# Decode pages taken in pairs, with another order of key and value pages beside the prompt

## The chip, the cores and the metric

The kernel runs on one core of one Trainium2 chip. The metric is device time in microseconds (us) of one execution; the figure shown is the median of the runs, and the lowest and highest beside it. A profile is one execution recorded instruction by instruction. The engines are PE (matrix multiply; PEld is its weight load), DVE (vector), ACT (activation), POOL (which also issues the gathers) and SP (which issues most other transfers).

## The reference

One step of a hybrid decoder layer for two groups that share the weights: a prompt of 1024 rows, and 8 samples of one row each with a cache of 8192 past positions in 64 pages of 128.

```python
# per layer, for the prompt (xp) and the samples (xs)
q, k, v, logf, u, z = mixer_inputs(rmsnorm(x, g_mix), w_in, b_f, g_sgu_v)
# prompt: causal attention with forget gates; samples: the same over the paged cache
s = einsum('bqhd,bkhd->bhqk', q, k) * HEAD_DIM ** -0.5 + (cq - ck)
att = einsum('bhqk,bkhd->bqhd', softmax(s), v)
x = x + concat(rmsnorm(att), rmsnorm(u * spatial(z))) @ w_o
# cross-attention, 4 heads of 256, into 256 memory rows (the samples' are cached)
x = x + cross_attend(rmsnorm(x, g_cross), mk, mv, w_cq, w_co)
# gated MLP with a causal convolution of width 3 over rows
h = rmsnorm(x, g_ffn) @ w_up
x = x + (silu(gate(conv(h))) * value(conv(h))) @ w_down
y = rmsnorm(x, g_final)
```

D_MODEL is 1024, there are 8 attention heads of 64 and D_FF is 2816. The outputs are both groups' rows, and the new keys, values, gates, memory keys and values and convolution states.

## The kernel before

Two streams of work are woven into one program. The first, `prompt()`, is a generator that goes through the prompt: `p1` (the input projection, and at its end the first loads of the attention), `attention(0)` beside the memory's keys and values (`pmem`) and the gating, `attention(1)`, and then for each half of 512 rows the merge, the output projection, the cross-attention (`cross`) and the MLP (`ffn`). Its large products are three whole-array matmuls each of 512 columns (`gemm3`, lines 271 to 273: high by high, high by low, low by high part). Weights come by SP into `wr`, ACT makes the high part `wh` (line 234) and DVE the low part `wl` (line 235).

The second stream, `sample()`, is the decode. `decode()` goes through the 8 samples' caches, 16 chunks each of 128 x 2048 numbers (1 MB), called pages here. A key page (`kstep`, line 1341) is gathered by POOL, multiplied by the query and summed on DVE (lines 1347 and 1351). When a sample's 16 key pages are done, its softmax follows (`soft_max`, `soft_all`, `soft_exp`, `soft_sum`). A value page (`vstep`, line 1400) is gathered by POOL, and PE multiplies it by the weights in four 32-column strips at once (line 1406). `sample_rest` then does the rest of the layer for the 8 rows, with weights and cached memory streamed as 1 MB pages too (`sample_proj`; cached keys and values at lines 1571 and 1606; `w_up` at 1652 with its matmuls at 1656; `w_down` at 1690 with its matmuls at 1695). All these pages share four buffers, `kv` (`NKV = 4`).

The loop at the end of `build` weaves the two: each step of `prompt()` yields an estimate of its PE time, and when the sum since the last decode step is over `PACE[phase]`, one step of the decode is emitted. `held[0]` stops that. A decode step in the order before is one key page and, one sample and two chunks behind, one value page; value pages are gathered one to a step and their matmuls emitted when two are pending (`VB = 2`). `behind(engine)` ties an instruction to come after the prompt's latest one on that engine. In the end a scheduler places the emitted instructions on the engines' in-order queues by what is ready and by order of emission, so that two pages emitted together need not stand together.

Of the kernel before, what the change touches and what calls it, by code (L numbers as in the profile page):

```python
# [18 lines left out]
P = 128  # L19
D = 1024  # L20
# [29 lines left out]

NKV = 4
VLAG = 2
VB = 2
MIXR = 1.0
G0R = 0.0
WH = 5
# [17 lines left out]
KS = 2  # L74
BKQ = 1
LA = (2, 2)
PACE = {'p1': 7.0, 'att0': 20.0, 'mid0': 8.0, 'ffn0': 8.5, 'att1': 15.0, 'mid1': 6.8, 'ffn1': 2.5, 'rest': 2.9}


def build(nc, tc, ctx, a, phases=None):  # L80
# [250 lines left out]
        return next(i for i in reversed(nc.cur_bb.bb.instructions) if i.engine == e)  # L331


    def p1(early):
        rstd = const.tile([P, 8], F32, tag="rstd", name="rstd")
        rstd8 = const.tile([P, 8], F32, tag="rstd8", name="rstd8")
# [203 lines left out]
        for tt in range(8):  # L540
            if tt < 4:
                ps = BK()
                mm_chunk(tt, ws, ps, 0, 512)
                if tt == SD - 1:
                    sps = [sample_copy(*sps[0])]
                if tt == SD:
                    sp = sample_sum(*sps[0])
                    zs = T2()[:8]
                    nc.scalar.activation(zs, sp, AF.Gelu_apprx_tanh, scale=rsk)
                    ssv = sm([8, 1], "sss", 1)  # L550
                    ssq_into(ssv, zs)
# [24 lines left out]
            nc.scalar.dma_start(zg_d[tt * P : (tt + 1) * P, :], z)  # L576
            yield 5.2 if tt < 4 else 0.1
# [104 lines left out]
    def attention(hf, late=None, at=3):  # L682
# [161 lines left out]
        for hp in range(4):  # L844
# [5 lines left out]
            for blk in range(2):  # L850
# [84 lines left out]
    def merge(att, sg):  # L935
# [12 lines left out]
        mh = mh[4:] + mh[:4]  # L948
        ml = ml[4:] + ml[:4]
        return mh, ml  # L950

    held = [False]

    def squares():
        return sm([P, 4, 2], "sqx", 2)
# [323 lines left out]
        yield 1  # L1279

    last = {}
    bgs, acc, phase = [], [0.0], ["p1", None]

    def behind(e):

# [3 lines left out]
    def decode():  # L1289
# [107 lines left out]
        def vstep(b, ch, st, dv):  # L1397
# [2 lines left out]
            nc.gpsimd.indirect_dma_start(kv, None, a["cache_v"], off(kidx[:, b, ch : ch + 1]))  # L1400
            kvv = kv.rearrange("p (k c) -> p k c", c=512)

            def mm():
                with behind(ENG.PE):
                    for j in range(4):
                        mmul(  # L1406
                            dv[32 * j : 32 * j + 32, :],
                            s[:, ch * 4 : ch * 4 + 4, :].rearrange("p k h -> p (k h)"),
                            kvv[:, j, :],
                            start=(ch == 0),  # L1410
                            stop=(ch == 15),
                            tile_position=(0, 32 * j),
                        )

# [21 lines left out]


        st, A, dt_, pm, dg, lp, dv, vm = ([None] * 8 for _ in range(8))
        pend = []
        st[0] = prep(0)  # L1440
        for g in range(8 * 16 + 16 + VLAG + 2):
            b, ch = divmod(g, 16)
            if ch == VLAG + 1 and 2 <= b < 10:
                vend(b - 2, vm[b - 2])
            if ch == 0 and 1 <= b < 9:
                dg[b - 1] = soft_all(b - 1, pm[b - 1])
            if ch == 1 and 1 <= b < 9:
                lp[b - 1] = soft_exp(b - 1, st[b - 1], dg[b - 1])
            if ch == 2 and 1 <= b < 9:
                soft_sum(b - 1, lp[b - 1])  # L1450
            if b < 8:
                kstep(b, ch, st[b])
# [8 lines left out]
            if len(pend) == VB:  # L1461

                for vb_, vch_, f in pend:
                    f()
                pend.clear()
                if vch_ == 15:
                    vm[vb_] = vmask(vb_, dv[vb_])
            vb, vch = divmod(g - 16 - VLAG, 16)
            if 0 <= vb < 8:
                if vch == 0:  # L1470
                    dv[vb] = DV()
                pend.append((vb, vch, vstep(vb, vch, st[vb], dv[vb])))
            yield 1


# [43 lines left out]
    def sample_rest(xs):  # L1519
# [81 lines left out]
            )  # L1601
        yield 1
        po = DV()
        for b in range(8):
            kv = KV().rearrange("p (a c) -> p a c", c=D)
            nc.gpsimd.dma_start(kv, a["cmv"][b].rearrange("(a p) c -> p a c", p=P))
            for n in range(2):
                for mt in range(2):
                    j = n * 2 + mt
                    mmul(po[32 * j : 32 * j + 32, :], pz[:, mt, b, :], kv[:, mt, n * 512 : (n + 1) * 512], start=(b == 0), stop=(b == 7), tile_position=(0, 32 * j))  # L1610
            yield 1
        vm = D2()
        nc.vector.tensor_tensor(
            vm.rearrange("p (h d) -> p h d", d=256),
# [28 lines left out]
        up = MS()  # L1643
        folds = []
        for f4 in range(11):
            ps = DV()
            for q in range(2):
                if q and folds:
                    folds.pop()()
# [3 lines left out]
                rv = raw.rearrange("p (f k c) -> p k f c", f=2, c=P)  # L1653
                for k in range(8):
                    j = k % 4
                    mmul(  # L1656
                        ps[32 * j : 32 * j + 32, q * 256 : (q + 1) * 256].rearrange("p (f c) -> p f c", f=2),
                        xsT[:, k, :],
                        rv[:, k],
                        start=(k < 4),  # L1660
                        stop=(k >= 4),
                        tile_position=(0, 32 * j),
                    )
                yield 1
            t = D2()
            nc.scalar.activation(t, ps, AF.Copy)

# [17 lines left out]
        nc.vector.tensor_tensor(g[:, :176], g[:, :176], hc[:, 176:352], op=ALU.mult)  # L1685
        yield 1
        ys = [DV(), MS()]
        for f2 in range(0, NF, 2):
            raw = KV().rearrange("p (f d) -> p f d", f=2)
            nc.gpsimd.dma_start(raw, a["w_down"][f2 * P : (f2 + 2) * P, :].rearrange("(f p) d -> p f d", p=P))  # L1690
            for q in range(2):
                f = f2 + q
                j = f % 4
                for n in range(2):
                    mmul(
                        ys[n][32 * j : 32 * j + 32, :],
                        g[:, f * 8 : f * 8 + 32],
                        raw[:, q, n * 512 : (n + 1) * 512],
                        start=(f < 4),
                        stop=(f >= NF - 4),  # L1700
                        tile_position=(0, 32 * j),
                    )
# [219 lines left out]
```

## Time and profile before

| | |
|---|---|
| median of 3 runs | 1874.07 us (1871.21 to 1876.5) |
| the profiled execution | 1881.57 us, its span 1879.7 us |
| mean granted TensorE clock | 0.982 |
| moved by DMA | 521.27 MB, mean 277 GB/s |

The span is from the first instruction to the last. A line of instructions reads: line of the kernel, engine, operation, tile written <- tiles read, shape, number, then total busy time, mean duration in ns, idle time of that engine just before such instructions, and what ended most of it. Matmuls overlap in the records, so the time that one costs is read from the start of one to the start of the next. Page matmuls are recorded as two instructions each.

### The profile page before, as it was taken

Reading aid. Unit: us, or ns where it says so; the run is one execution under the profiler, and the core shown is the slowest. Engines: PE = TensorE matmul, PEld = TensorE weight load, DVE = VectorE, ACT = ScalarE, POOL = GpSimd, SP = SyncE. Lnnn points to the kernel's source line nnn. Section 1 sums busy time; section 2 is a strip of 40 time slices with the busy share of each in tenths; the row PEclk is TensorE's granted clock in tenths of the full one; section 3 lists DMA queues with packets and bytes.
Section 4 is the critical chain, followed back from the end, with each engine's and each line's share of the span. In section 5 each row is a group of like instructions: output and inputs, shape, how many; then the busy total and the mean of one; then the engine's idle time right before and its main releaser. Section 6 shows DMA issues by size and latency. Waiting matters only on the chain.

```text
span 1879.7 us, 24248 instructions
## 1 busy us (share of the span) xinstructions
PE 1802.3 (96%) x9239; PEld 1291.7 (69%) x9239; DVE 1394.2 (74%) x1664; ACT 750.9 (40%) x1363; POOL 480.0 (26%) x437
## 2 busy tenths in 40 slices
PE   8999989878998999999999999999999999999998
PEld 5987666556676667776777776765675668667765
DVE  4788668776687787989989998897965549654344
ACT  6332356565633435333324234235353334232232
POOL 1232333331122332313422323334322111101110
PEclk9999999889998999999999999999999999999999
DMA  8877888784496876759877888889859577667971
GB/s 320 286 261 271 324 324 297 243 263 167 169 376 216 329 268 249 298 197 363 314 274 301 302 316 324 347 325 340 325 220 359 193 282 263 253 219 276 331 246 59
DMA packets 157012, 521.27 MB, mean 277 GB/s; under 512 B 20808, under 2 KB 40520, under 8 KB 124128
## 3 DMA queue, kind: packets, MB, share of 16 engines
q0 software_dynamic: 57168, 341.14, 49.1%
q1 hardware_dynamic: 92816, 165.99, 25.7%
q10 hardware_dynamic: 6912, 12.59, 1.8%
q8 instruction: 73, 1.20, 0.2%
q14 instruction: 43, 0.35, 0.1%
HBM read 495.73 MB, written 23.93 MB: 276 GB/s over the span
## 4 chain that ended last, share of the span: by engine, by line
PE 83%; DVE 5%; DMA 4%; ACT 3%; issue 3%; POOL 1%; SPq 0%; DVEq 0%; POOLq 0%; ACTq 0%
PE ba L271 13%; PE ba L272 12%; PE ba L273 12%; PE bb L271 7%; PE bb L272 7%; PE bb L273 7%; PE dv L1406 6%; DVE kv L1347 1%; PE dv L1656 1%; PE ba L1002 1%; PE ba L1004 1%; DMA kv<-cache_k,kidx 1%; PE bb L788 1%; DVE s L1351 1%; PE ba L1003 1%
## 5 line engine op out<-in xcount | busy, mean ns | idle before, releaser
L234 ACT ACTIVATE wh<-wr 128x1024 fp32r<-128x1024 f32 (+2 forms) x220 | 228.7, 1044 | 518.2 <-PE ba L272 168.5
L235 DVE TENSOR_TENSOR wl<-wr,wh 128x1024 fp32r<-128x1024 f32 (+2 forms) x220 | 262.8, 1200 | 134.0 <-PE ba L273 55.4
L1347 DVE TENSOR_TENSOR kv<-kv,d 128x1024 f32<-128x1024 f32 (+1 forms) x184 | 295.8, 1633 | 24.3 <-DMA kv<-cache_k,kidx 23.6
L1341 POOL DMA_INDIRECT kv<-cache_k,kidx x128 | 177.0, 1383 | 535.0 <-DVE s L1351 262.2
L1351 DVE TENSOR_REDUCE s<-kv 128x16 f32<-128x1024 f32 (+1 forms) x184 | 296.3, 1624 | 0.2
L1400 POOL DMA_INDIRECT kv<-cache_v,kidx x128 | 173.3, 1354 | 404.7 <-DVE s L1351 180.0
L271 PE MATMUL ba<-wh,u 128*128 128x512 f32 (+1 forms) x601 | 229.6, 383 | 4.3 <-DVE u L961 2.5
L272 PE MATMUL ba<-wl,u 128*128 128x512 f32 (+1 forms) x601 | 227.5, 379 | 0.0
L273 PE MATMUL ba<-wh,u 128*128 128x512 f32 (+1 forms) x601 | 224.9, 379 | 0.0
L272 PE MATMUL ba<-u,wh 128*128 128x512 f32 (+2 forms) x520 | 203.1, 391 | 0.0
L271 PE MATMUL ba<-u,wh 128*128 128x512 f32 (+2 forms) x520 | 202.7, 391 | 0.2 <-DVE u L238 0.2
L273 PE MATMUL ba<-u,wl 128*128 128x512 f32 (+2 forms) x520 | 202.1, 389 | 0.0
L271 PE MATMUL bb<-u,wh 128*128 128x512 f32 (+2 forms) x344 | 138.9, 404 | 1.1 <-DVE u L238 1.1
L271 PEld LDWEIGHTS ba<-wh,u 128*128 128x128 f32 x601 | 113.3, 189 | 38.2 <-issue 9.6
L272 PE MATMUL bb<-u,wh 128*128 128x512 f32 (+2 forms) x344 | 137.5, 401 | 1.6 <-DVE u L238 1.6
L1406 PE MATMUL dv<-kv,s 128*32 128x512 f32 x1024 | 135.2, 614 | 3.0 <-DMA kv<-cache_v,kidx 3.0
L273 PE MATMUL bb<-u,wl 128*128 128x512 f32 (+2 forms) x344 | 136.9, 398 | 0.0
L273 PEld LDWEIGHTS ba<-wh,u 128*128 128x128 f32 x601 | 113.0, 188 | 26.7 <-issue 5.0
L272 PEld LDWEIGHTS ba<-wl,u 128*128 128x128 f32 x601 | 113.3, 189 | 22.4 <-issue 1.7
L272 PEld LDWEIGHTS ba<-u,wh 128*128 128x128 f32 x520 | 98.5, 189 | 32.3 <-issue 12.2
L271 PEld LDWEIGHTS ba<-u,wh 128*128 128x128 f32 x520 | 98.3, 190 | 31.5 <-issue 8.4
L273 PEld LDWEIGHTS ba<-u,wl 128*128 128x128 f32 x520 | 98.2, 189 | 27.7 <-issue 8.1
(426 smaller groups left out, 3048.8 us busy)
## 6 DMA issues: line engine op xcount, KB each, us to landing
wr<-w_up SPq DMA_DIRECT2D x88, 512.0 KB
kv<-w_up POOLq DMA_DIRECT2D x22, 1024.0 KB
wr<-w_down SPq DMA_DIRECT2D x40, 512.0 KB
kv<-w_down POOLq DMA_DIRECT2D x11, 1024.0 KB
wr<-w_in SPq DMA_DIRECT2D x16, 512.0 KB
wr<-w_o SPq DMA_DIRECT2D x16, 512.0 KB
wr<-w_cq SPq DMA_DIRECT2D x16, 512.0 KB
wr<-w_co SPq DMA_DIRECT2D x16, 512.0 KB
```

The source lines that it names most:

```text
L234: nc.scalar.activation(h, src, AF.Copy)
L235: nc.vector.tensor_tensor(l, src, h.bitcast(F32), op=ALU.subtract)
L271: mmul(out, sh, mh, start=(i == 0), stop=False)
L272: mmul(out, sh, ml, start=False, stop=False)
L273: mmul(out, sl, mh, start=False, stop=(i == n - 1))
L788: nc.tensor.transpose(tr[:, c * P : (c + 1) * P], p_[:, kt * P : (kt + 1) * P], ident)
L1002: mmul(pss[i], mh[k][:, tb], wh, start=(k == korder[0]), stop=False)
L1341: nc.gpsimd.indirect_dma_start(kv, None, a["cache_k"], off(kidx[:, b, ch : ch + 1]))
L1347: nc.vector.tensor_tensor(kvv[:, i : i + m, :], kvv[:, i : i + m, :], qb.unsqueeze(1).broadcast_to((P, m, 512)), op=ALU.mult)
L1351: nc.vector.tensor_reduce(s[:, ch * 4 + i : ch * 4 + i + m, :].rearrange("p k h -> p (k h)"), kvv[:, i : i + m, :].rearrange("p k (h d) -> ...
L1400: nc.gpsimd.indirect_dma_start(kv, None, a["cache_v"], off(kidx[:, b, ch : ch + 1]))
L1406: mmul(dv[32 * j : 32 * j + 32, :], s[:, ch * 4 : ch * 4 + 4, :].rearrange("p k h -> p (k h)"), kvv[:, j, :], start=(ch == 0), stop=(ch == ...
```

## The change

- The decode no longer takes a key and a value page in each step. It counts key pages (`nk`) and value pages (`nv`) by themselves. In the phases named in `PATTERN` a letter chooses: `p1` takes keys alone, the first attention k v k k v, the second v v k (a v is a pair of value pages). In the other phases each step takes a key page and every second one also a pair of value pages.
- A pair's two gathers are issued in one step; in the next step the second page's matmuls are emitted, and the first page's tied to come right behind them (`first(newest(ENG.PE))`). The accumulation's start and stop move to chunks 1 and 14 to fit that order.
- `held[0]` is set at the projection's fifth tile of the last block, ahead of the attention's first loads, and cleared in the first attention at head pair 0, second block, first head, first row block, with the accumulated time set to 0. A `kstep` emitted while it is held is split in two.
- `PACE` is smaller in `p1` (6.3 for 7.0), `att0` (8.5 for 20), `ffn0` (8.0 for 8.5), `att1` (8 for 15) and `mid1` (6.7 for 6.8).
- In `sample_rest` the cached values, `w_up` and `w_down` are taken two pages at a time as well, the later first. For `w_down` all matmuls of one output half of both pages come together.

```diff
-VB = 2
+PATTERN = {'p1': 'k', 'att0': 'kvkkv', 'att1': 'vvk'}
+LINK = 1
-PACE = {'p1': 7.0, 'att0': 20.0, 'mid0': 8.0, 'ffn0': 8.5, 'att1': 15.0, 'mid1': 6.8, 'ffn1': 2.5, 'rest': 2.9}
+PACE = {'p1': 6.3, 'att0': 8.5, 'mid0': 8.0, 'ffn0': 8.0, 'att1': 8, 'mid1': 6.7, 'ffn1': 2.5, 'rest': 2.9}
...
                 if tt == 4:
+                    held[0] = True
                     early()
...
+                        if hf == 0 and (hp, blk, j, ii) == (0, 1, 0, 0):
+                            held[0], acc[0] = False, 0.0
...
-            def mm():
-                with behind(ENG.PE):
+            def mm(after=None):
+                with tc.issue_after(after) if after else behind(ENG.PE):
...
-                            start=(ch == 0),
-                            stop=(ch == 15),
+                            start=(ch == 1),
+                            stop=(ch == 14),
...
+        while nv < 128 or pend or ends:
+            k = nk < 8 * 16 + LINK + 3
+            v = nv < 128 and nk >= (nv // 16 + 1) * 16 + LINK + 2
+            if phase[0] in PATTERN:
+                p = PATTERN[phase[0]]
+                k = k and (not v or p[n % len(p)] == "k")
+                v = v and not k
+            elif n % 2:
+                v = False
+            if nk % 16 == 14 and nv - 2 * len(pend) < nk - 30:
+                k = False
+            n += 1
...
+            if k:
+                keys(*divmod(nk, 16))
+                nk += 1
+            if pend:
+                vb, vch, first, second = pend.pop()
+                second()
+                first(newest(ENG.PE))
...
+            if v:
+                vb, vch = divmod(nv, 16)
+                if vch == 0:
+                    dv[vb] = DV()
+                pend.append((vb, vch, *(vstep(vb, c, st[vb], dv[vb]) for c in (vch, vch + 1))))
+                nv += 2
             yield 1
...
+            for b in (b0 + 1, b0):
+                with tc.issue_after(newest(ENG.PE)) if b == b0 else nullcontext():
...
+            for q in (1, 0):
+                with nullcontext() if q else tc.issue_after(newest(ENG.PE)):
...
-        for f2 in range(0, NF, 2):
+        for f4 in range(0, NF, 4):
...
+            behind_ = None
+            for n in range(2):
+                for f2 in reversed(range(len(raws))):
+                    with tc.issue_after(behind_) if behind_ else nullcontext():
+                        for q in range(2):
+                            f = f4 + f2 * 2 + q
...
+                    behind_ = newest(ENG.PE)
```

`keys(b, ch)` is the old step's key part: the softmax steps of the sample before at chunks `LINK` to `LINK + 2`, then `kstep`, the gates at chunks 11 and 13, the next sample's query at 14 and `soft_max` at 15.

More of the change, by code (lines that the diff above doesn't have):

```diff
@@ L1281, in build @@
     last = {}
-    bgs, acc, phase = [], [0.0], ["p1", None]
+    bgs, phase = [], ["p1", None]
     def behind(e):
@@ L1438, in decode, with keys @@
         st, A, dt_, pm, dg, lp, dv, vm = ([None] * 8 for _ in range(8))
-        pend = []
+        pend, ends = [], []
         st[0] = prep(0)
[L1441 to L1445, printed above, removed]
+        nk = nv = n = 0
+        def keys(b, ch):
+            if ch == LINK and b:
                 dg[b - 1] = soft_all(b - 1, pm[b - 1])
-            if ch == 1 and 1 <= b < 9:
+            if ch == LINK + 1 and b:
                 lp[b - 1] = soft_exp(b - 1, st[b - 1], dg[b - 1])
-            if ch == 2 and 1 <= b < 9:
+            if ch == LINK + 2 and b:
                 soft_sum(b - 1, lp[b - 1])
@@ L1603, in sample_rest @@
         po = DV()
[L1604 to L1611, printed above, removed]
+        for b0 in range(0, 8, 2):
+            kvs = []
+            for b in (b0, b0 + 1):
+                kvs.append(KV().rearrange("p (a c) -> p a c", c=D))
+                nc.gpsimd.dma_start(kvs[-1], a["cmv"][b].rearrange("(a p) c -> p a c", p=P))
+            for b in (b0 + 1, b0):
+                with tc.issue_after(newest(ENG.PE)) if b == b0 else nullcontext():
+                    for n in range(2):
+                        for mt in range(2):
+                            j = n * 2 + mt
+                            mmul(
+                                po[32 * j : 32 * j + 32, :],
+                                pz[:, mt, b, :],
+                                kvs[b - b0][:, mt, n * 512 : (n + 1) * 512],
+                                start=(b == 1),
+                                stop=(b == 6),
+                                tile_position=(0, 32 * j),
+                            )
+            yield 2
         vm = D2()
@@ L1645, in sample_rest @@
         for f4 in range(11):
-            ps = DV()
+            ps, rvs = DV(), []
             for q in range(2):
-                if q and folds:
-                    folds.pop()()
                 raw = KV()
@@ L1652, in sample_rest @@
                 nc.gpsimd.dma_start(raw.rearrange("p (f d) -> p f d", f=2), a["w_up"][f : f + 2].rearrange("f p d -> p f d"))
[L1653 to L1664, printed above, removed]
+                rvs.append(raw.rearrange("p (f k c) -> p k f c", f=2, c=P))
+            if folds:
+                folds.pop()()
+            yield 1
+            for q in (1, 0):
+                with nullcontext() if q else tc.issue_after(newest(ENG.PE)):
+                    for k in range(8):
+                        j = k % 4
+                        mmul(
+                            ps[32 * j : 32 * j + 32, q * 256 : (q + 1) * 256].rearrange("p (f c) -> p f c", f=2),
+                            xsT[:, k, :],
+                            rvs[q][:, k],
+                            start=(k < 4),
+                            stop=(k >= 4),
+                            tile_position=(0, 32 * j),
+                        )
+            yield 1
             t = D2()
```

49 lines of the change are left out of this document (25 added, 24 removed).

## The prediction

> **What bounds the kernel now.** I read the page first: engines, granted clock, chain of waits.
>
> ```profile
> span 1879.7 us, 24248 instructions
> PE 1802.3 (96%) x9239; PEld 1291.7 (69%) x9239; DVE 1394.2 (74%) x1664; ACT 750.9 (40%) x1363; POOL 480.0 (26%) x437
> PEclk9999999889998999999999999999999999999999
> ...
> PE 83%; DVE 5%; DMA 4%; ACT 3%; issue 3%; POOL 1%; SPq 0%; DVEq 0%; POOLq 0%; ACTq 0%
> ```
>
> PE is busy for 96% of the span and holds 83% of the chain. So whatever PE no longer executes outside its idle stretches comes off the end, and whatever keeps it idle is added. The second view is busy time by stage: the projection after its start, the two attentions, the first gated MLP.
>
> ```profile
> 55.00:265.00 210.00, 209.92 (x1177) 164.32 (x1179) 170.28 (x136) 75.22 (x116) 67.77 (x50) 1.00 0.80 281
> 265.00:394.00 129.00, 109.59 (x596) 76.91 (x596) 98.08 (x151) 74.57 (x176) 38.01 (x47) 0.91 0.83 288
> 394.00:505.00 111.00, 96.76 (x647) 68.91 (x647) 76.10 (x109) 70.23 (x146) 25.58 (x30) 0.92 0.55 168
> 756.00:1130.00 374.00, 373.95 (x1736) 271.11 (x1736) 349.57 (x317) 129.28 (x199) 110.03 (x78) 1.00 0.81 299
> ```
>
> The columns are length, then busy time of PE, PEld, DVE, ACT and POOL, then granted clock, DMA share, GB/s. In the projection and the MLP PE has no idle time. In the two attentions it idles 129 - 109.59 + 111 - 96.76 = 33.7 us, and its clock is 0.91 and 0.92 there. A value page costs its full price in the first kind of stage and perhaps nothing in the second. The third view shows where those pages (8 records each, line 1406) stand now; its columns are the length, PE busy, PEld busy, clock and DMA.
>
> ```profile
> 0.00:265.00 265.00, 9.86 (x76) 2.03 (x80) 1.00 0.82 290
> 265.00:505.00 240.00, 13.82 (x104) 2.65 (x104) 0.91 0.70 233
> 505.00:756.00 251.00, 20.80 (x164) 4.08 (x166) 0.97 0.77 288
> 756.00:1130.00 374.00, 39.63 (x304) 6.98 (x304) 1.00 0.81 299
> 1130.00:1402.00 272.00, 32.35 (x240) 4.93 (x240) 0.99 0.86 321
> 1402.00:1480.00 78.00, 18.80 (x144) 3.05 (x144) 1.00 0.86 312
> ```
>
> That is 9.5, 13, 20.5, 38, 30 and 18 pages. In the instruction order of the built changed program, laid against the same places of the prompt's own matmuls, they stand 0, 20, 20, 40, 30 and 18.
>
> **The price of an interruption.** Page matmuls use 32-column strips, the prompt's use the whole array. The timeline of PE around one page alone, around two in a row, around a page of `w_up` and of `w_down`, and the first and last page stretch (start, length, instruction):
>
> ```profile
> 195.82 1.92 PE L1406 MATMUL dv<-kv,s 128*32 128x512 f32 x16
> ...
> 252.13 0.40 PE L437 MATMUL ba<-wh,u 128*128 128x512 f32 x1
> 252.45 1.92 PE L1406 MATMUL dv<-kv,s 128*32 128x512 f32 x16
> 254.31 0.50 PE L435 MATMUL ba<-wh,u 128*128 128x512 f32 x1
> 254.65 0.40 PE L436 MATMUL ba<-wl,u 128*128 128x512 f32 x1
> ...
> 1429.66 0.40 PE L271 MATMUL ba<-u,wh 128*128 128x512 f32 x1
> 1429.99 1.06 PE L1406 MATMUL dv<-kv,s 128*32 128x512 f32 x8
> 1430.99 0.50 PE L272 MATMUL ba<-u,wh 128*128 128x512 f32 x1
> 1431.32 0.39 PE L273 MATMUL ba<-u,wl 128*128 128x512 f32 x1
> 1431.55 0.40 PE L271 MATMUL ba<-u,wh 128*128 128x512 f32 x1
> ...
> 1468.52 1.07 PE L1406 MATMUL dv<-kv,s 128*32 128x512 f32 x8
> ...
> 1703.62 1.07 PE L1656 MATMUL dv<-kv,xsT 128*32 128x256 f32 x16
> ...
> 1797.61 1.06 PE L1695 MATMUL dv<-kv,d 128*32 128x512 f32 x4
> ...
> 1799.45 0.50 PE L273 MATMUL ba<-u,wl 128*128 128x512 f32 x1
> ...
> 1801.98 1.08 PE L1695 MATMUL dv<-kv,d 128*32 128x512 f32 x8
> ...
> 1803.85 0.50 PE L271 MATMUL ba<-u,wh 128*128 128x512 f32 x1
> ```
>
> Whole-array matmuls start 0.23 us apart (1431.32 to 1431.55). One page: from 1429.66 to 1431.32 are 1.66 us; without the two ordinary starts of 0.23 it is 1.20. Two pages: 252.13 to 254.65 are 2.52, less 0.46 is 2.06. So a page is 2.06 - 1.20 = 0.86 and an interruption 0.34 us.
>
> **The change, part by part.**
>
> *Pairs.* The 1024 records of line 1406 stand in 102 stretches, the first and last quoted above; most are of one page. The new code emits a pair's second page first and its first directly behind, so 64 stretches remain: 38 x 0.34 = 12.9 us. (The built order breaks some pairs with a small matmul of the decode itself; that costs no more than such a matmul does now.) A `w_up` page shows the same 1.07 us; its 21 stretches become 11: 3.4 us. The cross-attention's four single value pages become two pairs: 0.7. A single `w_down` page fills two of four strips: from 1797.61 to the next whole-array start are 1.84 us, for two pages in a row 1.87. Three single pages and four doubles, seven stretches, become five pairs and one single: one stretch less, 2.0 with its entry. Together 19.0. Bounds: nothing if pairs wait for their second page as long as they save; above 19 nothing.
>
> *Where the pages go.* With pairs priced, the projection loses 9.5 x 0.86 and 8 interruptions; the attentions gain 20.6 (20 x 0.86 + 10 x 0.34) - 13.6 (13 x 0.86 + 7 x 0.34) = 7.0 us of PE work. If all of that lengthened them, the 19.0 would be all. What falls into idle PE time is gain on top: 0 to 7.0, since 33.7 us are idle there. I take half, 3.5: the decode's matmuls stand in PE's fixed order, and only some meet a wait.
>
> *The pause.* From the last four projection tiles into the first attention no page is computed. The moment it touches (PE, ACT, and two windows):
>
> ```profile
> 276.95 0.48 PE L788 MATMUL bb<-cp,t 128*128 128x128 f32 x1 [5.72 <-ACT t L767]
> ...
> 273.45 1.06 ACT L234 ACTIVATE wh<-wr 128x1024 fp32r<-128x1024 f32 x1 [5.73 <-DMA wr<-w_ck]
> ...
> 265.00:275.00 10.00, 6.23 (x33) 4.26 (x33) 5.22 (x5) 4.14 (x9) 2.62 (x2) 0.95 1.02 410
> 275.00:285.00 10.00, 8.05 (x28) 6.50 (x29) 7.46 (x8) 4.40 (x10) 1.68 (x1) 0.71 0.94 355
> ```
>
> PE's longest gap, 5.72 us, is put down to the exponential at line 767, but ACT stood in order behind a weight split that waited 5.73 us for `w_ck`, with the DMA engines full (share 1.02, 410 GB/s). Then the clock is low: 10 x 0.05 + 10 x 0.29 = 3.4 us lost. In the built order POOL issues no page gather between the first head pair's setup and the second's, so `w_ck` no longer shares the queues with pages. Bounds 0 (another transfer is as late) and 5.7 + 3.4 = 9.1. What is late next is the exponential itself, behind its table load, so I take 7.0. The pause itself I cost at nothing: the denser pages of the attentions and the first MLP hide it, and in the built order the decode's last page stands within a few us of the same prompt matmul as before. Without that catching up, the decode's tail would end later by what it had lost, and the kernel with it once that tail passes the prompt's last tile.
>
> *Fewer keys in the attentions.* In program order 15 key pages stand on DVE there before, 11 after; the first MLP gets 40 in place of 37, the projection 30 in place of 28.
>
> ```profile
> L1347 DVE TENSOR_TENSOR kv<-kv,d 128x1024 f32<-128x1024 f32 (+1 forms) x184 | 295.8, 1633 | 24.3 <-DMA kv<-cache_k,kidx 23.6
> L1351 DVE TENSOR_REDUCE s<-kv 128x16 f32<-128x1024 f32 (+1 forms) x184 | 296.3, 1624 | 0.2
> ...
> 445.28 0.80 PE L760 MATMUL ba<-u,u 128*128 128x512 f32 x1 [1.27 <-ACT wr L770]
> ...
> 444.60:451.40 6.80, 6.12 (x24) 5.21 (x25) 3.76 (x6) 3.96 (x8) 0.00 (x0) 0.50 0.13 36
> ```
>
> A key page is (295.8 + 296.3)/128 = 4.63 us of DVE, so the attentions are spared 18.5 us on the engine that makes their row maxima. A softmax wait is short but dear: after the 1.27 us gap at 445.28 the clock is 0.50 for 6.8 us, 3.4 us lost. Bounds: 0 and four such gaps, 4 x (1.3 + 3.4) = 19. I credit one half-clock stretch, 3.4. The Trainium skill, "TensorE: Matmul & The Clock Gate", Part 1, says that the gate closes after an idle window of about 3.4 us; here a gap of 1.27 us was enough, so the measurement decides. By the rule only the 5.72 us gap would cost clock, this 3.4 would not exist, and the time would be 1845.
>
> In the first MLP three more key pages make DVE 349.6 + 13.9 = 363.5 of 374 us; PE's 374 us cover it. Without that cover it is the second rival. In the projection DVE goes from 170 to 179 of the 200 us that PE then needs, covered too.
>
> *Sum.* 19.0 + 3.5 + 7.0 + 3.4 = 32.9. The profiled execution took 1881.6 us (span 1879.7 and 1.9 around it): 1848.7. The runs' median, 1874.07, lies 7.5 below that execution, so 1841 by the median.
>
> **Rivals.**
>
> *Only the pairs count.* `w_ck` is late anyway, because its staging buffers come free late, and the added pages lengthen the attentions in full. For it: page gathers are not the only traffic before the gap. Against it: they are among that traffic now, and in the built order none remains. 1874.1 - 19.0 = 1855.
>
> *DVE becomes the bound in the first MLP.* DVE has 24.4 us of idle there now. If that idle is needed by its waits, 13.9 us more key work lengthens the stage by 13.9: 1855. Against it: PE shows no wait for DVE at 93%.
>
> *Slower: POOL's queue in the attentions.* The attentions' `cq_d`/`ck_d` loads and the key copies of the second attention are issued on POOL in order, and now more and doubled value gathers stand ahead of them; each waits for a buffer that a pair on PE frees, two pages later than a single one.
>
> ```profile
> POOL kv L1400 <- PE dv L1406: 175.6, 44, 17.0
> ```
>
> Such a wait is 175.6/44 = 4.0 us (longest 17.0). If each of the eight head-pair setups came 4.0 us late to PE and took a half-clock stretch of 3.4 with it: 8 x 7.4 = 59, and 1841 + 59 = 1900. It decides from five late setups on (5 x 7.4 = 37 against 32.9). Against it: a setup is emitted half a head pair ahead of its first use.
>
> **How the numbers follow.** The forecast, 1841, gets 0.50; only pairs 0.24; DVE bound 0.11; POOL's queue 0.12; the pages' positions changing nothing, with pairs that wait as long as they save, 0.03 (1874). About 0.3% (5.6 us) separates a change from none here. The first three cases are faster nearly whole: 0.82; same 0.06; slower 0.12. The forecast's own range: with no softmax credit and no filling 1848; with 9.1 for the pause, 7.0 filled and all 19 of the short gaps 1820. To hold eight in ten I take 1822 to 1866: it covers both 1855 cases with 11 us of misses and leaves out the queue case.
>
> **What would show it.** Pairs: line 1406's successor in about 64 stretches of x16, each about 2.06 us between the matmuls around it, and hardly any x8. The projection: the first score matmul some 10 us earlier, at about 255. The pause: no gap of 5 us at the start of the attentions, no wait of ACT for `w_ck`, clock above 0.95 there. The attentions: length under 235 us in place of 240, fewer half-clock stretches. Wrong would be: waits of PE for `cache_v` pages of 1 us and more at many pairs; waits for lines 725 or 741 growing in the attentions (the queue); waits of PE for DVE weight splits in the first MLP.

## The result and the profile after

The changed kernel takes 1892.51 us (median of 4 runs, 1887.82 to 1894.72) against 1874.28 us of the kernel before on the same chip: ratio 1.0087, 95% interval 1.0069 to 1.0104. It is slower by 18 us; the forecast was 1841, and even the range's upper end, 1866, is missed. From the page of the changed kernel, the lines that answer to those of before (engines, granted clock, chain of waits):

```profile
span 1888.9 us, 24222 instructions
PE 1797.9 (95%) x9239; PEld 1303.3 (69%) x9239; DVE 1392.1 (74%) x1660; ACT 750.4 (40%) x1363; POOL 504.4 (27%) x437
PEclk9999999899999999999999999989899999999999
...
PE 55%; DVE 9%; DMA 5%; issue 4%; ACT 1%; POOL 1%; POOLq 0%; DVEq 0%; SPq 0%; ACTq 0%
```

PE is busy 4.4 us less than before (1802.3), but stands idle 91.0 us of the span in place of 77.4. The shares of the chain cannot be compared as they stand: those here sum to 75%, because the chain could be followed back only to 469 us. From 470 us on PE holds 73% of it, before 85% over the same part. Of the dents in the clock one stands between 1228 and 1275 us and one between 1322 and 1369 us, where before there was none. The same windows as in the prediction, and two around the old gap for `w_ck` (columns as there):

```profile
55.00:265.00 210.00, 208.50 (x1137) 168.71 (x1136) 178.70 (x142) 81.23 (x129) 67.38 (x43) 1.00 0.77 270
265.00:394.00 129.00, 109.79 (x624) 76.31 (x623) 94.63 (x152) 73.19 (x174) 38.67 (x49) 0.92 0.78 261
394.00:505.00 111.00, 101.93 (x698) 66.74 (x697) 67.00 (x102) 69.99 (x143) 28.58 (x34) 0.97 0.66 223
756.00:1130.00 374.00, 370.11 (x1725) 271.14 (x1724) 350.29 (x315) 122.35 (x190) 133.47 (x80) 0.99 0.81 302
265.00:275.00 10.00, 7.29 (x37) 5.12 (x35) 5.72 (x9) 7.43 (x18) 3.18 (x4) 1.00 0.62 211
275.00:285.00 10.00, 7.85 (x29) 6.50 (x30) 3.31 (x5) 5.19 (x10) 1.99 (x4) 0.66 0.35 108
```

The pages stand nearly where the built order said (line 1414, 8 records a page: 0, 22, 20 and 38), and most come in pairs: the 1024 records stand in 75 stretches (102 before, 64 forecast). The two lower lines are a pair of value pages and a pair of `w_up` pages on PE's timeline:

```profile
0.00:265.00 265.00, 0.00 (x0) 0.00 (x0) 1.00 0.80 281
265.00:505.00 240.00, 24.48 (x176) 4.87 (x176) 0.94 0.73 243
505.00:756.00 251.00, 22.36 (x160) 4.52 (x160) 0.97 0.74 276
756.00:1130.00 374.00, 39.49 (x304) 8.51 (x304) 0.99 0.81 302
...
1426.16 1.92 PE L1414 MATMUL dv<-kv,s 128*32 128x512 f32 x16
...
1715.86 1.93 PE L1703 MATMUL dv<-kv,xsT 128*32 128x256 f32 x32
```

**Where the time went.** The prompt's own matmuls are the same in both kernels, so they serve as milestones. I took those that stand within 6 us of 150, 282, 505, 756, 1160, 1345, 1640 and 1845 us in the profile of before, looked up the same ones in another profile, and took the median of their shifts. The change of a stage's length between two milestones is the table's entry (before: 132, 223, 251, 404, 185, 295 and 205 us; good to about 1 us, but for the one at 1160, see e9 to e12). Each row is one profiled execution, up to 8 us from the median of its kernel (e6: 1882.55 against 1874.85), and leaves out what comes before 150 us (up to 5.4 us, e6) and behind 1845 us (up to 7.0, e3), so that a row need not add up to the ratio. Ratios are to the kernel before on the same chip, with their 95% intervals; the change, e1 to e4, e5 to e8, e9 to e12 and e13 to e15 were each measured as a group beside it, the four groups of experiments on four chips.

| kernel | ratio | 150: projection, pause | 282: attentions | 505: first merge, cross-att. | 756: first MLP | 1160: second merge, cross-att. | 1345: second MLP | 1640: tail |
|---|---|---|---|---|---|---|---|---|
| the change | 1.0087 (1.0069 to 1.0104) | -16.9 | +10.3 | -0.6 | +14.0 | +12.6 | -4.9 | -6.6 |
| e1 pairs in the tail | 0.9971 (0.9952 to 0.9990) | +0.2 | -0.2 | -1.1 | 0.0 | +1.4 | -1.9 | -7.2 |
| e2 decode pairs | 1.0015 (1.0001 to 1.0030) | -8.4 | +10.4 | +0.7 | -2.3 | -1.9 | +0.8 | +0.1 |
| e3 pause | 1.0096 (1.0059 to 1.0133) | -11.7 | +5.8 | -6.8 | -2.6 | -5.3 | +18.0 | +6.1 |
| e4 single gathers | 0.9902 (0.9875 to 0.9929) | -18.0 | +15.1 | -7.7 | +5.4 | +2.9 | -6.1 | -6.8 |
| e5 wider steps | 1.0022 (1.0002 to 1.0043) | -18.0 | +11.4 | -0.6 | +0.6 | +8.0 | +4.6 | -9.0 |
| e6 key between | 0.9982 (0.9968 to 0.9995) | -18.0 | +14.6 | -3.8 | +4.5 | -5.4 | +5.0 | -1.6 |
| e7 pause, faster | 1.0008 (0.9999 to 1.0016) | -12.2 | +5.2 | +2.3 | +6.2 | -3.8 | -3.3 | +3.5 |
| e8 values in projection | 1.0050 (1.0035 to 1.0065) | -12.1 | +18.1 | -1.3 | +0.3 | -2.4 | -0.5 | -3.3 |
| e9 the change, shift 3 | 1.0008 (0.9992 to 1.0023) | -18.0 | +21.8 | -9.6 | +12.2 | +10.4 | -8.2 | -9.6 |
| e10 the change, shift 5.5 | 0.9983 (0.9965 to 1.0002) | -18.0 | +13.4 | -3.4 | +17.9 | -0.3 | -5.5 | -9.2 |
| e11 single, shift 3 | 1.0001 (0.9983 to 1.0019) | -18.0 | +21.8 | -3.9 | +3.5 | +3.8 | -4.4 | -8.4 |
| e12 single, shift 5.5 | 0.9964 (0.9945 to 0.9983) | -18.0 | +12.6 | -11.7 | +10.1 | -2.9 | +4.5 | -9.2 |
| e13 single, wide | 0.9963 (0.9947 to 0.9978) | -18.0 | +11.3 | -6.2 | -2.3 | +5.7 | +0.4 | -5.9 |
| e14 between, wide | 0.9956 (0.9941 to 0.9972) | -18.0 | +10.7 | -3.3 | -4.5 | -0.1 | -0.5 | -3.5 |
| e15 single, wide, shift 5.5 | 0.9989 (0.9977 to 1.0000) | -18.0 | +13.4 | -11.1 | -2.2 | +0.1 | +18.3 | -10.1 |

So the change gains up to 282 us nearly what was forecast for the projection and the pause, and it gains in the tail. It loses 10 us in the attentions, 14 in the first MLP and 13 in the second cross-attention. Three places show how.

*The attentions.* The windows between the milestones 282 and 505, first all instructions, then line 1406 or 1414 alone, before and after:

```profile
282.00:505.00 223.00, 195.07 (x1196) 137.50 (x1195) 164.50 (x248) 137.14 (x307) 59.28 (x74) 0.92 0.68 219
...
282.00:505.00 223.00, 12.84 (x96) 2.58 (x96) 0.92 0.68 219
```

```profile
266.10:499.40 233.30, 205.02 (x1282) 138.78 (x1281) 157.09 (x245) 138.30 (x307) 65.62 (x82) 0.94 0.72 242
...
266.10:499.40 233.30, 22.72 (x171) 4.73 (x172) 0.94 0.72 242
```

PE idles 223 - 195.07 = 27.9 us before and 233.3 - 205.02 = 28.3 after. The value pages' time rises by 22.72 - 12.84 = 9.9, the stage by 10.3. That looks as if the added pages had been paid in full, but the stage's two parts say otherwise. The first part, up to the matmuls of 345 us, before and after, and the wait of its longest gap after:

```profile
282.00:345.00 63.00, 58.64 (x317) 42.67 (x316) 52.11 (x67) 37.93 (x81) 18.94 (x24) 0.97 0.88 309
```

```profile
266.06:336.00 69.94, 61.36 (x320) 44.28 (x319) 46.55 (x64) 38.34 (x81) 17.81 (x23) 0.95 0.71 241
...
277.15 1.11 PE L709 MATMUL ba<-cp,t 128*128 128x128 f32 x4 [3.04 <-DMA t<-q_d]
```

Four value pages stand in this part in both kernels, and yet it is 6.9 us longer: PE idles 8.6 us in place of 4.4, with more half clock. SP issues the load of `q_d` at 270.51 us, behind loads of `w_cv`, 12.9 us earlier than before, while the prompt was 15.9 us early. So the pause wins 8.8 us between the matmuls of 265 and 282 us, and 7.2 of them are lost again by those of 310; in e4 to e6 and e9 to e15, which start alike, 8.8 and 5.3 to 7.8. The second part, 345 to 505, is 3.4 us longer with 9.4 pages more, which are 9.1 us of PE: there most of the added pages did fall into idle time.

*The end of the first MLP.* The chain of waits of the changed kernel there:

```profile
1130.83 0.60 DVE u L238
1131.43 0.66 DVE t L1232
1132.08 1.13 DVE wl L238
1133.21 2.20 DVE kv L1355
1135.42 0.66 DVE t L1231
...
1138.10 0.61 DVE t L1238
...
1138.77 7.63 DMA t<-sgn_d
...
1147.87 18.31 DMA u<-an_d
```

The chain lies on DVE, instruction after instruction, a key page's multiply (2.20 us) among the prompt's. Behind `t` of line 1238 SP could load `sgn_d`, and PE waited 1.66 us for it. The loads of `an_d` were issued 8.6 us later, behind other loads of SP; the last took 18.31 us, and PE waited 3.9 us for them. From 1140 to 1170 us PE was idle for 7.9 us; in the profile of before for 0.2 us from 1130 to 1160, and for 2.5 us up to 1166. The fastest version, e4, waits 5.69 us for the same `an_d`, so this wait does not come from the doubled value gathers.

*The softmax of the second cross-attention.* POOL, DVE, ACT and PE around PE's longest gap:

```profile
1306.05 5.23 POOL L1349 DMA_INDIRECT kv<-cache_k,kidx  x1 [1.71 <-DVE cmx L1120]
...
1311.65 2.43 DVE L1355 TENSOR_TENSOR kv<-kv,d 128x1024 f32<-128x1024 f32 x2 [1.19 <-DMA kv<-cache_k,kidx]
...
1319.38 2.36 DVE L1355 TENSOR_TENSOR kv<-kv,d 128x1024 f32<-128x1024 f32 x2 [5.22 <-DMA kv<-cache_k,kidx]
1322.79 0.68 DVE L1119 TENSOR_REDUCE cmx<-ba 128x2 f32<-128x512 f32 x1
1324.52 0.68 DVE L1119 TENSOR_REDUCE cmx<-ba 128x2 f32<-128x512 f32 x1
...
1327.37 0.23 DVE L1120 TENSOR_TENSOR cmx<-cmx,rq 128x2 f32<-128x2 f32 x2
1327.56 0.56 ACT L1123 ACTIVATE u<-ba,cmx,rq 128x256 f32<-128x256 f32 x1 [8.38 <-DVE cmx L1120]
...
1328.81 3.78 PE L1117 MATMUL ba<-t,u 128*128 128x256 f32 x8 [8.91 <-ACT u L1123]
```

POOL takes 5.23 us over one key gather; DVE, in order, stands 5.22 us before that page's multiply, with the prompt's row maxima (line 1119) behind it; ACT stands 8.38 us and PE 8.91. The clock is at half from within this gap, 1323.5 us, to 1333.7.

### The profile page after: what moved, and what is told of

It is laid out like the page before. It is cut to its first block, busy times and chain, and to the rows that moved or that the text cites. A ratio compares the mean times of both kernels' runs of the same rounds, so it can differ in the third digit from the quotient of the medians.

```text
span 1888.9 us, 24222 instructions
## 1 busy us (share of the span) xinstructions
PE 1797.9 (95%) x9239; PEld 1303.3 (69%) x9239; DVE 1392.1 (74%) x1660; ACT 750.4 (40%) x1363; POOL 504.4 (27%) x437
## 4 chain that ended last, share of the span: by engine, by line
PE 55%; DVE 9%; DMA 5%; issue 4%; ACT 1%; POOL 1%; POOLq 0%; DVEq 0%; SPq 0%; ACTq 0%
PE ba L274 8%; PE ba L275 8%; PE ba L276 8%; PE bb L274 4%; PE bb L276 4%; PE bb L275 4%; PE dv L1414 4%; DVE kv L1355 2%; DVE s L1359 2%; DMA kv<-cache_k,kidx 2%; DVE wl L238 1%; PE ba L1010 1%; PE ba L1011 1%; PE dv L1703 1%; PE ba L1012 1%
## 5 line engine op out<-in xcount | busy, mean ns | idle before, releaser
L1349 POOL DMA_INDIRECT kv<-cache_k,kidx x128 | 215.8, 1686 | 549.4 <-DVE s L1359 313.3
L1355 DVE TENSOR_TENSOR kv<-kv,d 128x1024 f32<-128x1024 f32 (+1 forms) x182 | 295.2, 1651 | 39.5 <-DMA kv<-cache_k,kidx 35.3
L1408 POOL DMA_INDIRECT kv<-cache_v,kidx x128 | 166.9, 1304 | 349.8 <-PE dv L1414 254.6
L275 PEld LDWEIGHTS ba<-u,wh 128*128 128x128 f32 x520 | 99.6, 192 | 34.2 <-issue 10.7
```

What stands on the lines that cost most here:

```text
L275: mmul(out, sh, ml, start=False, stop=False)
L1349: nc.gpsimd.indirect_dma_start(kv, None, a["cache_k"], off(kidx[:, b, ch : ch + 1]))
L1355: nc.vector.tensor_tensor(kvv[:, i : i + m, :], kvv[:, i : i + m, :], qb.unsqueeze(1).broadcast_to((P, m, 512)), op=ALU.mult)
```

## The experiments

Each edit is given against the kernel that its first line names; ratios and stages are in the table above.

**e1, pairs in the tail alone.** Edit: in the kernel before, `sample_rest` takes cached values, `w_up` and `w_down` as the change does.

```diff
+        for b0 in range(0, 8, 2):
...
+            for q in (1, 0):
...
+        for f4 in range(0, NF, 4):
```

> The kernel before, with the pairs of the last part alone (cached values, w_up, w_down two pages at a time); the decode as before. Theory A (an interruption of PE costs 0.34 us and pairs save it; the loss of the change comes from the decode's new order of key and value gathers): 6 to 10 us under before, 1864 to 1868. Theory B (a pair waits for its second page as long as it saves): 1874 or more, with waits of PE for kv pages at w_up or w_down.

Measured: 1873.24 us, 0.9971; the kernel before took 1880.02 beside it, so it is 6.8 us less, within theory A's 6 to 10. The milestones are within 2 us until 1640 and then 7 to 9 us early. Pairs in the tail pay.

**e2, pairs in the decode alone.** Edit: in the kernel before, gathers still alternate, but the two pending value pages stand together, the later first.

```diff
-                for vb_, vch_, f in pend:
-                    f()
+                pend[1][2]()
+                vb_, vch_, f = pend[0]
+                f(newest(ENG.PE))
```

> The kernel before, its order of key and value gathers kept (k v k v), but the two pending value pages are emitted the later first and the earlier tied right behind. Theory A: about 102 stretches become about 64, some 10 us less: 1862 to 1868. Theory B: no gain or a loss, 1874 or more, with PE waiting for cache_v pages.

Measured: 1882.33 us, 1.0015. Its page:

```profile
PE 1792.3 (95%) x9239; PEld 1299.9 (69%) x9239; DVE 1392.2 (74%) x1664; ACT 750.7 (40%) x1363; POOL 487.4 (26%) x437
```

PE is busy 1802.3 - 1792.3 = 10.0 us less, which is the saving, and the span is still 1879.4: PE is idle 9.7 us more. The time is theory B's, but its sign is not there: PE has no wait for `cache_v` pages. At the start of the attentions waits have moved across the milestone of 282 us (ACT waits 4.66 us for `w_ck` at 278 us, PE 3.04 us for `q_d` at 292), so the -8.4 before it and the +10.4 behind it, with 12 value pages as before, belong together. In the first MLP, with 42 pages as before, PE is busy 3.7 us less and 2.3 us came off.

**e3, the pause alone.** Edit: in the kernel before, `held[0]` set and cleared as in the change.

```diff
                 if tt == 4:
+                    held[0] = True
                     early()
...
+                        if hf == 0 and (hp, blk, j, ii) == (0, 1, 0, 0):
+                            held[0], acc[0] = False, 0.0
```

> The kernel before, with the pause alone (decode held from the fifth tile of the last projection block to the first attention's second block). Theory A: the 5.7 us gap of PE at the start of the attentions and its half clock go, 5 to 9 us less: 1865 to 1869. Rival (the decode that is held back comes back where it is dearer): 1874 or more though the gap is gone.

Measured: 1896.41 us, 1.0096. The prompt is 11 us early at 282 us and 20 at 1345, and it loses that, and more, behind 1480 us. The timeline of this run where most is lost:

```profile
1608.79 0.50 PE L272 MATMUL ba<-wl,u 128*128 128x512 f32 x1 [1.47 <-DVE wl L235]
1609.26 4.62 DVE L1579 TENSOR_TENSOR kv<-kv,d 128x1024 f32<-128x1024 f32 x4
...
1616.78 1.22 PE L273 MATMUL ba<-wh,u 128*128 128x512 f32 x2 [3.68 <-DVE u L235]
...
1625.30 0.79 PE L271 MATMUL ba<-wh,u 128*128 128x512 f32 x1 [5.58 <-DVE u L1259]
```

The decode, held back and not sped up, is late: its last value page is read at 1505 us (1470 before). So its cached-key multiplies (line 1579) meet the second MLP's element-wise steps, which they had passed before: three gaps, 10.7 us, and half clock in and behind them (0.73 from 1616 to 1635 us).

**e7, the pause, with a decode that catches up.** Edit to e3:

```diff
-'mid0': 8.0, 'ffn0': 8.5, 'att1': 15.0, 'mid1': 6.8,
+'mid0': 7.5, 'ffn0': 7.9, 'att1': 15.0, 'mid1': 6.5,
```

> The kernel before with the pause alone, as in the run that came to 1.0096, but with the decode's steps closer afterwards (first cross-attention 7.5 instead of 8.0, first MLP 7.9 instead of 8.5, second cross-attention 6.5 instead of 6.8), so that it has caught up when its last stage begins. Theory T (the pause saves its 7 us, and the other run lost them again because the late decode met the norm and the tiles at 1609 to 1625 us): 0.992 to 0.997, and the PE gaps between 1600 and 1630 us sum to under 3 us instead of 10.7. Rival (a pause, or a decode that must be denser later, costs more than the gap it removes): 1.003 or more.

Measured: 1880.51 us, 1.0008. The window from 1600 to 1660 us, in e3 and here:

```profile
1600.00:1660.00 60.00, 48.53 (x207) 34.25 (x209) 46.33 (x63) 15.14 (x21) 8.85 (x13) 0.91 0.72 249
```

```profile
1600.00:1660.00 60.00, 59.04 (x279) 40.24 (x278) 35.50 (x58) 18.65 (x25) 7.32 (x10) 1.00 0.69 260
```

The gaps are gone and 16 us are back: a late decode was the cause of e3. But the pause's own gain does not reach the end either, and the ratio lies between the two forecasts. With the denser steps the first MLP is 6.2 us longer and the stage before it 2.3.

**e4, one value gather per step.** Edit to the change: outside the projection and the attentions POOL gathers key, value, key, value; the pairs on PE stay.

```diff
-            elif n % 2:
-                v = False
+            many = 2 if phase[0] in PATTERN else 1
...
+                for _ in range(many):
+                    if len(pend) < 2:
```

> The changed kernel, but outside the projection and the attentions one value gather in each step after the key's (k v k v on POOL) in place of a key, two values, a key; pairs on PE as changed. Theory A (a key gather that stands behind two value gathers, which wait for PE, reaches DVE late, and the prompt's DVE work stands behind it): DVE's wait for key pages falls from 35 us to below 24, the waits in the second half's cross-attention go, 1892 becomes 1870 to 1880. Rival C (the loss comes from more key work at the same places, by the smaller PACE, not from POOL's order): 1888 to 1896.

Measured: 1862.93 us, 0.9902, the fastest of all and faster than both kernels. Over the whole run DVE's waits for key pages are no fewer (38.5 us; 35.3 in the change), so that sign failed. In the first MLP, between the milestones, they are; the waits there, of the change and of e4:

```profile
DVE kv L1355 <- DMA kv<-cache_k,kidx: 9.9, 6, 4.4
DVE kv L1355 <- issue: 3.3, 1, 3.3
```

```profile
DVE kv L1355 <- DMA kv<-cache_k,kidx: 4.6, 6, 1.8
```

That is 13.2 (with the 3.3 for which the profile shows no cause) against 4.6 us, and the stage is 418.0 against 409.4 us.

**e5, wider steps.** Edit to the change:

```diff
-'ffn0': 8.0, 'att1': 8, 'mid1': 6.7,
+'ffn0': 8.5, 'att1': 8, 'mid1': 6.8,
```

> The changed kernel, with the decode's steps in the first MLP 8.5 apart instead of 8.0 and in the second half's cross-attention 6.8 instead of 6.7, as before the change; all else of the change stays. Theory G (two value gathers in a row hold the next key gather back on POOL, the key page comes late to VectorE, and the prompt behind it): stays near 1.0087 of before, 1.004 to 1.012, with the losses near 841, 1232 to 1251 and 1329 us in place. Theory D (the denser steps alone crowd VectorE): comes to 0.990 to 0.994, and those gaps go. Theory P (which key step meets which short chain of the prompt is a matter of alignment): anywhere between, with other gaps in other places.

Measured: 1881.47 us, 1.0022: between the theories. The gap at 841 us is gone and the first MLP is 13.4 us shorter, but a gap of 6.26 us, for a load of `o_mk`, stands at 1310 us now. Its own executions go from 1871.59 to 1890.31 us.

**e6, a key gather between the two value gathers.** Edit to the change:

```diff
+            early = v and k and not pend
+            if early:
...
+                first_ = vstep(vb, vch, st[vb], dv[vb])
             if k:
                 keys(*divmod(nk, 16))
```

> The changed kernel, where outside the projection and the attentions the key gather is issued between the two value gathers of its step (v k v, k on POOL instead of k v v, k), so that no key gather has two value gathers right ahead of it; pairs on TensorE, spacing and everything else as in the change. Theory G: 0.989 to 0.994 of before, as with one value gather per step (0.990). Theory D: stays at 1.004 to 1.012. Theory P: anywhere between, with gaps in other places.

Measured: 1874.85 us, 0.9982: again between.

**e8, values back in the projection.** Edit to e4: the pattern for `p1` is taken out, and its spacing is 7.0 again.

```diff
-PATTERN = {'p1': 'k', 'att0': 'kvkkv', 'att1': 'vvk'}
+PATTERN = {'att0': 'kvkkv', 'att1': 'vvk'}
...
-'p1': 6.3,
+'p1': 7.0,
```

> The version with one value gather per step (0.990 of before), but with the decode's values back in the projection (spacing 7.0, alternating as before the change). If keys alone in the projection are worth the 9 us by which the prompt was ahead at 250 us: 0.995. If the value pages moved from there to the attentions are paid there in full, as the lead lost between 275 and 500 us suggests: 0.990, within 0.002, and the lead at 500 us is equal in both.

Measured: 1887.51 us, 1.0050. Neither: the projection is 6 us longer than in e4, and the attentions, with fewer pages (19 for 21.4), still 3 us longer. Up to 505 us keys alone in the projection are worth the 9 us; the rest of the 0.0148 between e8 and e4 arises later, and e9 to e12 tell how little that says.

**e9 to e12, a shift.** Edit to the change (e9, e10) and to e4 (e11, e12); one number, 3.0 or 5.5:

```diff
-                            held[0], acc[0] = False, 0.0
+                            held[0], acc[0] = False, 3.0
```

> The changed kernel, whose decode takes up its steps after the pause 3.0 us of its count earlier: the same steps, order of gathers and spacing, only shifted against the prompt. Theory G (order of the gathers) and theory D (spacing) alike: as the change, 1.004 to 1.012 of before, with short PE gaps still summing to 10 us or more more than before. Theory P (which key step meets which short chain of the prompt decides): anything from 0.990 to 1.010, with the gaps at 841, 1146 to 1166, 1232 to 1251 and 1329 us gone or in other places.

> The same with a shift of 5.5. Theories G and D: 1.004 to 1.012. Theory P: anything from 0.990 to 1.010, and apart from the run shifted by 3.0 by more than 0.003.

> The version with one value gather per step (0.990 of before), its decode shifted by 3.0 in the same way. Theory G: 0.987 to 0.994, all versions with single gathers below all versions with double ones. Theory P: 0.988 to 1.005, as likely as not among the times of the shifted changed kernels.

> The same with a shift of 5.5. Theory G: 0.987 to 0.994. Theory P: 0.988 to 1.005.

Measured: 1.0008 and 0.9983 for the change, 1.0001 and 0.9964 for e4's version. A few us of shift, with the same work, order and spacing, move the whole by up to 1%. So theory P holds for the total, though e9 and e10 lie 0.0025 apart and not the 0.003 it had named: most of what made the change 1.0087 rather than 0.998, and e4 0.990 rather than 1.000, is place, as far as ratios from different chips can be compared. The order of gathers counts too, but less. At the three places it is worth 0.0185, 0.0007 and 0.0019. In the first MLP it has the same sign each time: 418.0 against 409.4 us, 416.2 against 407.5, 421.9 against 414.1, that is 8.6, 8.7 and 7.8. These are rougher than they look, since the shift jumps by up to 8 us right at the milestone of 1160: with one at 1150 they are 9.1, 7.6 and 12.0, with one at 1175 8.1, 8.9 and 5.4. DVE's waits for key pages there are 13.2 against 4.6, 12.7 against 8.8, and 24.1 against 11.7 us.

**e13 to e15, wider steps with the other orders.** Edit to e4 (e13), e6 (e14) and e12 (e15):

```diff
-'ffn0': 8.0,
+'ffn0': 8.5,
```

> The version with one value gather per step, and the decode's steps in the first MLP 8.5 apart as before the change instead of 8.0. Theory V (VectorE is the bound there, and each denser key step or late key page is paid): the stage between the prompt's matmuls of 756 and 1160 us takes 401 to 405 us (409 with one gather per step at 8.0; 418 in the change; 404 before); the end at 0.986 to 0.994. Theory P (place alone): the stage anywhere from 402 to 415, the end from 0.988 to 1.003.

> The version with the key gather between the two value gathers, with 8.5 in the first MLP. Theory V: the stage 401 to 405 us (408.5 at 8.0), the end 0.990 to 0.997. Theory P: the stage anywhere from 402 to 415, the end from 0.990 to 1.005.

> As the first of these, the decode shifted by 5.5 after the pause. Theory V: the stage 401 to 406 us again (414 at 8.0 with this shift), whatever the end, which the other stages set: 0.988 to 1.000. Theory P: the stage longer than 407.

Measured: 0.9963, 0.9956 and 0.9989. The first MLP, between its milestones, in the change and in e13, in the usual columns:

```profile
749.80:1167.80 418.00, 406.23 (x1905) 294.92 (x1905) 391.17 (x359) 144.17 (x225) 149.40 (x90) 0.99 0.82 307
```

```profile
744.00:1145.70 401.70, 401.70 (x1888) 294.03 (x1887) 378.30 (x349) 142.41 (x223) 121.84 (x84) 1.00 0.81 305
```

The stage takes 401.7, 399.5 and 401.8 us, whatever the order and the shift, and 404.6 with doubled gathers (e5); at 8.0 the change and e4, e6 and e9 to e12 took 407 to 422 (e8, with values in the projection, 404.3). That is theory V's stage, with e14 1.5 us under its range; of the ends, e13's lies above theory V's 0.994. DVE reduces 41 key pages in the stage at 8.5, and 42 to 44 at 8.0. The work kept out is done later: e13 gains 7.7 us here over e4 and is not faster in total, where e4 met a good place. In e15 the late decode meets the second MLP as in e3 (+18.3).

## Why the prediction failed

*What held.* The page positions, nearly. The pairs in part: 27 stretches fewer in the place of 38. The projection, to the matmuls of 265 us: 10.9 forecast, 8.0 measured in the change and 9.1 in most of its versions. ACT no longer waits for `w_ck`. The tail: 6.1 forecast, 6.6 measured, 7.2 in e1. The condition put on the pause (that the decode catches up) held in the change, and e3 shows the loss without it.

*The first sentence of the argument failed:* that whatever PE no longer executes comes off the end. e2 is the plain case: 10.0 us fewer on PE, 9.7 more idle. The new idle time is spread: 1.5 us net up to 505 us, 1.4 in the first MLP, 3.9 in the second cross-attention and the rest in small pieces. PE holds 81% of e2's chain, nearly as before, so that share did not tell what a saving was worth. What PE waits for instead was not isolated in e2. In the tail the sentence holds (e1).

*"PE's 374 us cover it" failed.* This was the second rival's condition, given 0.11. DVE was busy 374.2 of 404 us between the first MLP's milestones before, and 391.2 of 418 after (the row above); the row of before:

```profile
756.00:1160.00 404.00, 403.78 (x1886) 291.57 (x1886) 374.20 (x346) 143.54 (x224) 118.91 (x84) 1.00 0.81 302
```

PE idles 11.8 us in the stage in place of 0.2. The idle time goes with the key pages: 0.0 to 2.7 us with 41 (e5, e13 to e15), 3.1 to 14.4 with 42 to 44 in the other versions of the change; e7, with 43 in the old order, idles 0.9 and is longer by PE's own work. The rival's price, 13.9 us, is what the stage lost (14.0), but that is partly chance, since the runs divide it otherwise than the rival did: some 8 us go with doubled value gathers, behind which key pages come late (e4, e11, e12 against the change, e9, e10). The rest goes with the number of steps (e13 to e15). That DVE, and not another wait, takes the rest is argued from its busy time and its waits; `an_d` above is a wait of another kind. The Trainium skill, "Perfetto Trace Analysis", Optimization Strategy, says that the most-contended engine can change over a kernel's regimes. The trace agrees: after the change DVE is busy 391.2 of 418 us here, and 157.1 of 233.3 in the attentions.

*The pause's 7.0 was mis-sized: 1.7 came.* "What is late next is the exponential itself, behind its table load" was wrong. Next is the load of `q_d`, 3.04 us, and the clock falls again (0.66 from 275 to 285 us), so that 7.2 of the 8.8 us won up to 282 us are lost by 310. The lower bound that the prediction gave this term, 0 if another transfer is as late, was the nearer one.

*"I take half, 3.5" is not refuted, but nothing steady came of it.* From 310 us to 505 the change is 3.1 us longer with 9.4 pages more, where the sum had almost nothing; other versions with this pattern lose 3.3 to 14.6 there with 7 to 10 pages more. Why they differ stays open. The credit for fewer half-clock stretches, 3.4, is there in the clock (0.92 to 0.94 of 233 us is about 4.7) but not to be told apart in the length.

*The slower rival was in the wrong place.* POOL's queue did hold something up, yet key pages for DVE in the later stages, and not head-pair setups in the attentions. In the second cross-attention, too, doubled gathers are the longer in all three pairs, by 9.7, 6.6 and 2.6 us, as rough as the numbers at that milestone are. The 9 us that the sum had left for the later decode stages (32.9 less 10.9 and 7.0, the tail's 6.1 and the attentions' -0.1) became a loss of 21: -0.6, +14.0, +12.6, -4.9. These 30 us, the pause's 5.3, the projection's 2.9 and the attentions' 3.0 make 41 of the 42 us between the forecast for a profiled execution (1848.7) and the one measured (1890.7).

*What the forecast could not have held.* 0.8 to 1.0% of the change's time hangs on where the decode's steps fall against the prompt (e9, e10). The three places of the changed kernel average 1.0026: as far as three places tell, as a design it is about as fast as before. What stays open is which single meetings of steps make a place good; e4's place was found, not designed, and its two shifts give 1.0001 and 0.9964.

## What to carry to other kernels

An engine's share of the chain of waits does not price a saving on it: compare the engines stage by stage before counting one, and test a stage by its milestones rather than the whole by its time. A wait that is removed may come back some 20 us later as the next one, so set the second milestone well behind it, and look whether the shift is steady where a milestone stands. Where two streams are woven, shift one against the other and run it several times before believing in a difference of a per cent, and check that the background stream still ends where it did.

## What the runs showed of the hardware

Half clock after a short gap again: behind the gap of 2.51 us that ends at 841.3 us of the change the clock is at half for 7 us. At the gap of 8.91 us that ends at 1328.8 it is at half for 10 us, from 5 us before the gap's end on. The windows (last but two: the clock):

```profile
842.20:849.10 6.90, 5.73 (x22) 1.54 (x20) 6.90 (x11) 1.06 (x1) 3.10 (x3) 0.51 0.91 331
1323.50:1333.70 10.20, 4.89 (x16) 2.93 (x20) 6.60 (x12) 5.91 (x17) 1.87 (x2) 0.50 0.71 256
```

And a page gather's time on POOL varies much, as far as the profile's rough spans on POOL tell: in the change 134 of 256 take under 1 us, one took 6.52 (6.88 is the longest before), and the key gathers' mean rose from 1383 ns to 1686 with the change, with the same 128 gathers:

```profile
L1349 POOL DMA_INDIRECT kv<-cache_k,kidx x128 | 215.8, 1686 | 549.4 <-DVE s L1359 313.3 <-PE dv L1414 101.7 <-ACT junk L232 32.2
...
1141.17 6.52 POOL L1349 DMA_INDIRECT kv<-cache_k,kidx  x1 [2.69 <-DVE s L1359]
```
